# Norms two and four of a hybrid decoder step: squares in two parts, a root on ScalarE, state updates in other chunks, y in pairs

## The chip, the core and the metric

The kernel runs on one core of one Trainium2 chip. The core has a matrix engine (TensorE, PE in the profile, with its weight loads as PEld), VectorE (DVE), ScalarE (ACT), GpSimd (POOL) and SyncE (SP). Each takes its instructions in a fixed order from its own queue, and they wait for each other by semaphores; SP, ACT and POOL also issue DMAs. The metric is the device time of one execution in microseconds (us).

## The reference

One layer of a decoder: two residual blocks, each with a norm before and a norm after. 256 prompt tokens and 64 sample tokens (8 sequences of 8) run together as NT = 320 columns. What matters here:

```
def rms_norm(x, w):
    y = xf * lax.rsqrt(jnp.mean(xf * xf, axis=-1, keepdims=True) + EPS)
    return y * w

h    = rms_norm(x, norm_mix_pre)                                  # norm one
mix  = concat(gate_out, ssm_out) @ w_out
x    = x + rms_norm(mix, norm_mix_post)                           # norm two
f    = conv_ffn(rms_norm(x, norm_ffn_pre), ..., w_up, w_down)     # norm three
x    = x + rms_norm(f, norm_ffn_post)                             # norm four, x is the output y
```

`ssm_out` comes from a state space mixer with four groups of heads, which also returns its states: one of the prompt, and one renewed state for each of the 8 sample sequences (`state * decay + outer products of the new tokens`). All of it is float32.

## The kernel before

**Layout.** Activations lie transposed: 16 blocks of 128 features (KD = 16), each 128 partitions by 320 tokens. A float32 product is done as three products of rounded parts (`accumulate`, lines 126 to 130): weight high times activation high (L128), weight high times activation low (L129), weight low times activation high (L130). Weights come in slabs of 512 KB (`slab`, L110): a DMA on SP's queue, a cast to the high half `whi` on ScalarE (L117), and the low half `wlo` on VectorE (L119), each with three buffers.

**Order of the work.** A planner lists the instructions of each engine ahead of time from its own estimate of durations and from priorities. `first()` gives a block the highest priority, slabs come next, and the rest follows the order in which it is written. `tc.issue_after(ins)` puts those instructions of a block that run on the engine of `ins` behind `ins` in that engine's queue. It orders the queue and adds no wait on other engines.

**Stages.** The input projection and both mixers run first. `chunk_out` (L198) adds a chunk of four blocks of a second product into the accumulator: per output block, 12 matmuls and one DVE addition (L210). `w_out` has 8 chunks, numbered 0 to 7, and a chunk takes some 28 us of TensorE. Between pairs of blocks it calls `tick`, `rate` times, which advances work from a list `bg` of generators: the head groups' state work (`ssd`), the norm of a group (`norm` in `heads_out`) and, with chunk 7, the last states.

**Norm two** (lines 967 to 986). `squares_of(sq2)` is called after each block of chunk 7: for blocks 0 to 12 ScalarE squares the block (L259) and POOL adds it to the total (L260); for blocks 13 to 15 ScalarE writes the square to PSUM (L274) and DVE adds it (L272, L276). `token_sums` (L236) sums the total over partitions with three small matmuls against ones (each is two passes), `rsqrt_of` (L219) finds the inverse root on DVE from a bit trick and three Newton rounds (11 instructions of three columns), `spread` (L245) turns the result into rows for all partitions with three transposes. Between the last matmul of chunk 7 and the sums stands `final`, the prompt state of group 3 (two passes on TensorE, L902; sum on DVE, L903; DMA on ScalarE's queue).

**The last sample states** (`renewals`, L810, group 3). For each of four steps i, two states: loads on SP (L713), `picked` on ScalarE (L793), `renewed` with POOL's products (L798), two matmuls (L802) and two DVE sums (L803), and `store_state` with two DMAs on ScalarE's queue (L808). The first two steps run with chunk 7, the third is issued around the sums of norm two, the fourth behind the up projection's first part.

**x1 and norm three** (lines 987 to 1016). `x1_ready` makes the new x block by block: scale by norm two (L1001, DVE), add the old x (L1002; DVE for the first two blocks, POOL after), split into `h_hi` (L320, ScalarE) and `h_lo` (L321, DVE). The up projection starts as blocks come; besides its 512 columns it takes 256 more from the other half (`more`) with two further PSUM banks. Squares for norm three are made on ScalarE and added in turn by POOL (`sq3`) and DVE (`sq3b`). They are read by `token_sums(sq3, sq3b)` (L1078), which TensorE meets between the halves of `ps_one`.

**Norm four and y** (lines 1100 to 1149). The last chunk of `ffn_w_down` calls `last`, which squares as above and scales the block (L1107). After the sums, `hand_over` copies x1 blocks into PSUM through TensorE with an identity (L1129, two passes a block), so that DVE can add them from there. `r4` is the spread in PSUM and `r4s` its copy in SBUF. Eight pairs of blocks follow: five on DVE, three (5, 6, 7) on POOL, and DMAs to y that take turns on SP's and ScalarE's queues.

Of the kernel before, what the change touches and what calls it, by code (L numbers as in the profile page):

```python
# [34 lines left out]
def hybrid_step(  # L35
# [116 lines left out]
    def project(w, c0, evac, width=512, spare=False, late=None, quiet=0, ready=None, small=0, after=None, ahead=1, rate=1, more=None):  # L152
# [26 lines left out]
        for i, (k0, nk) in enumerate(cuts):  # L179
            with tc.issue_after(there or after) if there or after and i > 1 else nullcontext():  # L180
                if ready and i + ahead < len(cuts):
                    there = ready(*cuts[i + ahead])
                if nk < 4:
                    part(rows_of(w, k0, nk, c0, 512), k0, nk, range(4))
                    if more and k0 % 4 == 2:
                        part(rows_of(w, k0 - 2, 4, more, 256), k0 - 2, 4, (4, 5))
# [48 lines left out]

    def token_sums(*sqs):  # L236
# [25 lines left out]
    def squares_of(total):  # L262

        held = []

        def step(nb):
            if nb < KD - 3:
                add_square(total, acc[:, nb, :], nb == 0)
                return
            with first():  # L270
                if held:
                    dve.tensor_tensor(out=total, in0=total, in1=held.pop(), op=ALU.add)  # L272
                held.append(misc("sq_ps")[:, :NT])
                act.activation(held[0], acc[:, nb, :], AF.Square)  # L274
                if nb == KD - 1:
                    dve.tensor_tensor(out=total, in0=total, in1=held.pop(), op=ALU.add)  # L276
        return step
# [61 lines left out]
    with ExitStack() as mctx:  # L339
# [336 lines left out]
        with tc.tile_pool(name="sd", bufs=1) as sd:  # L676
# [26 lines left out]
            def ssd(g):  # L703
# [92 lines left out]
                def renewed(i, st, bm):  # L796
                    for h in range(2):
                        pool.tensor_tensor(out=by_head(st[h]), in0=by_head(st[h]),  # L798
                                           in1=tote[:, h0:h0 + 8, 4 * h + i:4 * h + i + 1].to_broadcast([P, 8, 64]), op=ALU.mult)
                    for h in range(2):  # L800
# [5 lines left out]
                def store_state(i, st):  # L806
                    for h in range(2):
                        act.dma_start(o_ssm_s[4 * h + i, g], st[h])  # L808

                def renewals():  # L810
                    sts = [load_state(i) for i in range(2)]
                    yield
                    for i in range(4):
                        st = sts.pop(0)
                        made = renewed(i, st, picked(i))
                        if i == 2:
                            yield made
                        elif i < 2:
                            yield
                        store_state(i, st)  # L820
                        if i < 2:
                            sts.append(load_state(2 + i))

                for i in range(4):
# [6 lines left out]
                    if g < 3:  # L831
                        renewed(i, st, bm)
# [67 lines left out]
                def final():  # L900
                    ps = misc("fin_ps")
                    made = pe.matmul(ps, btok[:, 1, bs], x1d, start=True, stop=True)  # L902
                    dve.tensor_tensor(out=s1, in0=s1, in1=ps, op=ALU.add)  # L903
# [330 lines left out]
```

## Time and profile before

| what | us |
|---|---|
| median of 3 runs (1817.86, 1818.88, 1823.92) | 1818.88 |
| the profiled execution's own time | 1820.49 |
| its span, first to last instruction | 1818.8 |
| TensorE matmul busy | 1784.2 (98%) |
| VectorE busy | 1181.1 (65%) |
| ScalarE busy | 790.5 (43%) |
| GpSimd busy | 300.3 (17%) |
| PE idle from 470 to 780 | 6.4 |
| PE idle from 850 to 865 | 7.2 |
| PE idle from 1800 to the end | 11.5 |

"Busy" is the time in which the engine had an instruction of the program running; the idle time before an instruction is put down to what released it. PE's busy time counts matmuls in flight, and the granted clock stands beside it in the windows: at half clock a busy PE does half the work. The profile shows 24 loads of ScalarE's function tables (ACT_TABLE_LOAD), 1283 ns each; the last two are at 757.72 us (for SiLU) and at 923.41 us (for GELU).

### The profile page before, as it was taken

What the parts mean: (1) busy time and instruction counts of PE and PEld (TensorE: products, weight loads), DVE (VectorE), ACT (ScalarE), POOL (GpSimd) and SP (SyncE); (2) the same over time, 40 slices, a digit from 0 to 9 for tenths busy, and PEclk for the clock granted to TensorE, in tenths of its full rate; (3) what the DMA queues carried; (4) which work ended last, traced back from release to release, by engine and by line L of the source; (5) the groups of instructions that cost most, each with busy time, mean ns of one, the idle gap of its engine ahead of it and who ended that gap; (6) DMA issues with size and microseconds to landing.
All of it is one profiled execution on the core that took longest, in us unless ns stands there. A gap on an engine that the chain in (4) does not pass through costs nothing.

```text
span 1818.8 us, 31127 instructions
## 1 busy us (share of the span) xinstructions
PE 1784.2 (98%) x12189; PEld 1746.0 (96%) x12189; DVE 1181.1 (65%) x2046; ACT 790.5 (43%) x1094; POOL 300.3 (17%) x623
## 2 busy tenths in 40 slices
PE   8999999999999999998999999999999999999997
PEld 7999999999889799997999999999999999999996
DVE  4449664557977868676776465747566575656575
ACT  5444454334535445444554433333434343433334
POOL 2102200000331302103521010111101020101004
PEclk9999999999999999999999999999999999999999
DMA  8646545555566565555454545454445444454542
GB/s 266 187 141 185 174 133 152 156 155 176 201 190 190 171 190 176 151 170 180 150 161 152 152 151 152 152 153 152 153 150 154 146 154 146 154 150 152 151 154 93
DMA packets 222994, 294.65 MB, mean 162 GB/s; under 512 B 16736, under 2 KB 150464, under 8 KB 222656
## 3 DMA queue, kind: packets, MB, share of 16 engines
q1 hardware_dynamic: 210256, 269.72, 48.6%
q10 hardware_dynamic: 10448, 16.10, 2.4%
q0 software_dynamic: 2144, 6.85, 1.3%
q8 instruction: 96, 1.57, 0.4%
q14 instruction: 50, 0.41, 0.1%
HBM read 277.80 MB, written 14.82 MB: 161 GB/s over the span
## 4 chain that ended last, share of the span: by engine, by line
PE 87%; DVE 5%; DMA 3%; POOL 2%; ACT 1%; issue 1%; POOLq 0%; SPq 0%; ACTq 0%; DVEq 0%
PE ps L128 18%; PE ps L129 18%; PE ps L130 18%; PE pd L128 9%; PE pd L130 9%; PE pd L129 9%; DVE wlo L119 2%; DMA st<-in_state_ssm 1%; DMA cT<-in_x_tok 1%; PE y_ps L876 1%; ACT whi L117 1%; POOL acc_mix L1002 1%; DVE cs L861 0%; PE sg L640 0%; DVE cv L363 0%
## 5 line engine op out<-in xcount | busy, mean ns | idle before, releaser
L119 DVE TENSOR_TENSOR wlo<-wraw,whi 128x1024 fp32r<-128x1024 f32 (+1 forms) x474 | 588.0, 1241 | 448.2 <-ACT whi L117 445.5
L117 ACT CAST whi<-wraw 128x1024 fp32r<-128x1024 f32 (+1 forms) x474 | 494.1, 1043 | 727.0 <-PE ps L129 428.2
L128 PE MATMUL ps<-h_hi,whi 128*128 128x320 f32 x2528 | 787.5, 312 | 6.6 <-ACT whi L117 3.7
L130 PE MATMUL ps<-h_hi,wlo 128*128 128x320 f32 x2528 | 784.1, 310 | 3.5 <-DVE wlo L119 3.5
L129 PE MATMUL ps<-h_lo,whi 128*128 128x320 f32 x2528 | 783.3, 310 | 0.0
L128 PEld LDWEIGHTS ps<-h_hi,whi 128*128 128x128 f32 x2528 | 477.3, 189 | 12.0 <-ACT whi L117 4.4
L130 PEld LDWEIGHTS ps<-h_hi,wlo 128*128 128x128 f32 x2528 | 477.1, 189 | 5.7 <-DVE wlo L119 5.6
L129 PEld LDWEIGHTS ps<-h_lo,whi 128*128 128x128 f32 x2528 | 477.2, 189 | 0.7 <-issue 0.5
L130 PE MATMUL pd<-fhi,wlo 128*128 128x320 f32 x704 | 217.4, 309 | 0.0
L128 PE MATMUL pd<-fhi,whi 128*128 128x320 f32 x704 | 217.4, 309 | 0.0
L129 PE MATMUL pd<-flo,whi 128*128 128x320 f32 x704 | 217.4, 309 | 0.0
L128 PE MATMUL pd<-ohi,whi 128*128 128x320 f32 x448 | 140.2, 313 | 0.0
L129 PE MATMUL pd<-olo,whi 128*128 128x320 f32 x448 | 138.9, 310 | 0.0
L130 PE MATMUL pd<-ohi,wlo 128*128 128x320 f32 x448 | 138.6, 309 | 0.0
L128 PEld LDWEIGHTS pd<-fhi,whi 128*128 128x128 f32 x704 | 132.2, 188 | 0.0
L129 PEld LDWEIGHTS pd<-flo,whi 128*128 128x128 f32 x704 | 132.2, 188 | 0.0
L130 PEld LDWEIGHTS pd<-fhi,wlo 128*128 128x128 f32 x704 | 132.2, 188 | 0.0
L1056 POOL COPY ptf<-pad 128x2 f32<-128x2 f32 x88 | 21.1, 240 | 598.0 <-DVE pad L1044 597.5
L210 DVE TENSOR_TENSOR acc_ffn<-acc_ffn,pd 128x320 f32<-128x320 f32 x160 | 77.4, 484 | 38.8 <-PE pd L130 37.4
L128 PEld LDWEIGHTS pd<-ohi,whi 128*128 128x128 f32 x448 | 84.1, 188 | 2.8 <-issue 1.6
L130 PEld LDWEIGHTS pd<-ohi,wlo 128*128 128x128 f32 x448 | 84.1, 188 | 1.0 <-issue 1.0
L129 PEld LDWEIGHTS pd<-olo,whi 128*128 128x128 f32 x448 | 84.1, 188 | 0.4 <-issue 0.2
(286 smaller groups left out, 1582.6 us busy)
## 6 DMA issues: line engine op xcount, KB each, us to landing
wraw<-in_ffn_w_up SPq DMA_DIRECT2D x176, 512.0 KB, 3.7
wraw<-in_w_in SPq DMA_DIRECT2D x144, 512.0 KB, 3.7
wraw<-in_ffn_w_down SPq DMA_DIRECT2D x88, 512.0 KB, 3.5
wraw<-in_w_out SPq DMA_DIRECT2D x64, 512.0 KB, 3.5
st<-in_state_ssm SPq DMA_DIRECT2D x40, 256.0 KB, 3.8
out_ssm_state_sample<-st ACTq DMA_DIRECT2D x32, 256.0 KB, 3.6
cs<-dacs_d SPq DMA_DIRECT2D x16, 320.0 KB, 4.4
xr<-in_xT SPq DMA_DIRECT2D x4, 640.0 KB, 4.8
```

The lines of the kernel that those rows point to most:

```text
L117: act.copy(hi[:, :m], raw[:, :m])
L119: dve.tensor_tensor(out=lo[:, :m], in0=raw[:, :m], in1=hi[:, :m].bitcast(F32), op=ALU.subtract)
L128: pe.matmul(ps, whi, xhi, start=first, stop=False)
L129: pe.matmul(ps, whi, xlo, start=False, stop=False)
L130: return pe.matmul(ps, wlo, xhi, start=False, stop=last).ins
L210: dve.tensor_tensor(out=acc[:, nb, :], in0=acc[:, nb, :], in1=ps[:, :NT], op=ALU.add)
L876: pe.matmul(ps[64 * i:64 * i + 64, cols], w(hl), x(hl, m, cpx), tile_position=(0, 64 * i), **flags)
L1002: added.append((dve if kt < 2 else pool).tensor_tensor(out=a, in0=a, in1=xr[q][:, k, :], op=ALU.add).ins)
L1056: pool.tensor_copy(ptf[:, k, :], pad[:, 256:258])
```

## The change

It has five parts.

- **Squares.** `squares_of` now returns its step and a list `one`. Blocks 13 and 14 are squared into PSUM and added by DVE; the square of block 15 goes to an SBUF tile of its own. The sums over partitions are taken in two goes: first of the 15 blocks, then of the last block alone.
- **Root.** `rsqrt_by_root` takes the two sums: two DVE steps make mean plus EPS, ScalarE takes the square root, DVE the reciprocal, and one Newton round follows (three DVE steps). A first `Sqrt` of one column stands behind the square of block 0, so that the table is loaded there.
- **States.** `renewed` is split into `shrunk` (POOL) and `grown` (TensorE, DVE), with a tick between. Steps 0 and 1 run with chunk 6, step 2 and the products of step 3 with chunk 7; the matmuls of step 3 come right behind chunk 7 and its stores go out by POOL's queue. `final` is a generator: its matmul comes behind the sums, its DVE sum behind the root, its store (group 3) goes out by POOL's queue.
- **Third norm.** All sums of squares are on DVE, in one total `sq3`. The `more` slabs' DVE work stands behind the second x1 block (`held`).
- **y.** x1 blocks 0 to 10 are handed over and done on DVE, in pairs and one after the other, and go out by SP; blocks 11, 12 to 13 and 14 to 15 are done on POOL and go out by ScalarE's queue. `r4s` comes from a second spread.

```diff
+        with tc.issue_after(held[1]):
+            part(rows_of(w, k0 - 2, 4, more, 256), k0 - 2, 4, (4, 5))
...
+    def rsqrt_by_root(rest, ps, scale, rows=P):
...
+        dve.tensor_scalar(out=v, in0=rest, scalar1=scale, scalar2=EPS, op0=ALU.mult, op1=ALU.add)
+        dve.scalar_tensor_tensor(out=v, in0=ps, scalar=scale, in1=v, op0=ALU.mult, op1=ALU.add)
+        act.activation(s, v, AF.Sqrt)
+        dve.reciprocal(r, s)
+        dve.scalar_tensor_tensor(out=t, in0=v, scalar=-0.5, in1=r, op0=ALU.mult, op1=ALU.mult)
+        dve.tensor_tensor(out=t, in0=t, in1=r, op=ALU.mult)
+        rsqrt_ins.append(dve.scalar_tensor_tensor(out=r, in0=t, scalar=1.5, in1=r, op0=ALU.add, op1=ALU.mult).ins)
+        return r
...
     def squares_of(total):
-        held = []
+        one, held = [], []
         def step(nb):
             if nb < KD - 3:
                 add_square(total, acc[:, nb, :], nb == 0)
+                if nb == 0:
+                    act.activation(tp.tile([P, 1], F32, name="root_there", bufs=1), total[:, 0:1], AF.Sqrt)
                 return
             with first():
-                if held:
-                    dve.tensor_tensor(out=total, in0=total, in1=held.pop(), op=ALU.add)
-                held.append(misc("sq_ps")[:, :NT])
-                act.activation(held[0], acc[:, nb, :], AF.Square)
-                if nb == KD - 1:
-                    dve.tensor_tensor(out=total, in0=total, in1=held.pop(), op=ALU.add)
-        return step
+                if nb < KD - 1:
+                    held.append(misc("sq_ps")[:, :NT])
+                else:
+                    one.append(tp.tile([P, NT], F32, tag="sq", name="sq", bufs=2))
+                act.activation((one or held)[-1], acc[:, nb, :], AF.Square)
+                if nb > KD - 3:
+                    dve.tensor_tensor(out=total, in0=total, in1=held.pop(0), op=ALU.add)
+        return step, one
...
                 def renewals():
                     sts = [load_state(i) for i in range(2)]
                     yield
                     for i in range(4):
+                        st, bm = sts.pop(0), picked(i)
+                        shrunk(i, st)
+                        yield
+                        made = grown(st, bm)
+                        store_state(i, st, act if i < 3 else pool)
                         if i < 2:
                             sts.append(load_state(2 + i))
+                        yield made
...
             finish(norm)
+            bg.append(chain(repeat(None, 1), islice(rest[0], 4)))
             chunk_out(w_out, 6, *res[2], False, rate=2)
...
-            bg.append(chain(repeat(None, 4), islice(rest[0], 2)))
-            chunk_out(w_out, 7, *res[3], False, squares_of(sq2))
+            bg.append(islice(rest[0], 3))
+            squares, one = squares_of(sq2)
+            chunk_out(w_out, 7, *res[3], False, squares)
...
                 with tc.issue_after(pd_last[-1]):
-                    made = rest[1]()
+                    made = next(rest[0])
                 with tc.issue_after(made):
-                    ps = token_sums(sq2)
-                r = rsqrt_of(ps, 1.0 / D, 3)
+                    most = token_sums(sq2)
+                with tc.issue_after(sums_ins[-1]):
+                    ps = token_sums(*one)
+                with tc.issue_after(sums_ins[-1]):
+                    made = next(rest[1])
+                r = rsqrt_by_root(most, ps, 1.0 / D)
                 behind = rsqrt_ins[-1]
                 with tc.issue_after(behind):
-                    made = next(rest[0])
+                    next(rest[1])
...
-            project(ffn_w_up, 0, None, late=up0, ready=x1_ready, after=behind, ahead=1, more=DFF)
-            sq3b = tp.tile([P, NT], F32, tag="pv", name="sq3b", bufs=4)
-            with tc.issue_after(added[11]):
+            project(ffn_w_up, 0, None, late=up0, ready=x1_ready, after=behind, ahead=1, more=DFF, held=added)
+            with tc.issue_after(added[15]):
                 for kt in range(KD):
-                    add_square((sq3, sq3b)[kt % 2], acc[:, kt, :], kt < 2, (pool, dve)[kt % 2], ("pv", 4))
-            with tc.issue_after(behind):
-                for _ in rest[0]:
-                    pass
+                    add_square(sq3, acc[:, kt, :], kt < 1, dve, ("pv", 4))
...
-        r = rsqrt_of(token_sums(sq4), 1.0 / D, 3)
-        hand_over((mm, "mm"), 0, 1)
+        with tc.issue_after(pd_last[-1]):
+            most = token_sums(sq4)
         with tc.issue_after(sums_ins[-1]):
-            hand_over((mm, "mm"), 2, 3)
-        r4 = spread(r)
-        r4s = fp.tile([P, NT], F32, name="r4s")
-        act.copy(r4s, r4)
+            made = hand_over(banks, 0)
+        with tc.issue_after(made):
+            ps = token_sums(*one)
+        r = rsqrt_by_root(most, ps, 1.0 / D)
+        with tc.issue_after(sums_ins[-1]):
+            made = hand_over(banks, 1, 2)
+        with tc.issue_after(made):
+            r4 = spread(r)
+            r4s = fp.tile([P, NT], F32, name="r4s")
+            spread(r, r4s)
+        hand_over(banks, 3)
+        hand_over(more, 4, 5)
+        hand_over(banks, 6, 7, 8, 9, 10)
+        made = None
+        for ks in [slice(k, k + 2) for k in range(0, 10, 2)] + [slice(10, 11)]:
...
+            with tc.issue_after(made) if made else nullcontext():
+                dve.tensor_tensor(out=f, in0=f, in1=r4.unsqueeze(1).to_broadcast([P, n, NT]), op=ALU.mult)
+            for k in range(n):
+                made = dve.tensor_tensor(out=f[:, k, :], in0=f[:, k, :], in1=x1p[ks.start + k], op=ALU.add).ins
+            sp.dma_start(o_y[:, ks, :], f)
+        for ks in (slice(11, 12), slice(12, 14), slice(14, 16)):
...
+            pool.tensor_tensor(out=f, in0=f, in1=r4s.unsqueeze(1).to_broadcast([P, n, NT]), op=ALU.mult)
+            pool.tensor_tensor(out=f, in0=f, in1=x1[:, ks, :], op=ALU.add)
+            act.dma_start(o_y[:, ks, :], f)
```

59 lines of the change are left out of this document (25 added, 34 removed).

## The prediction

> **What bounds the kernel now.** I read the page first, then the windows, the chain of waits, and each engine's timeline where TensorE is not full. The page gives TensorE 98% of the span (1784.2 of 1818.8 us), so a change can win only where it idles or runs at a low clock. The windows show two such places (columns: stretch and its length; busy us and instructions of PE, PEld, DVE, ACT, POOL; granted clock; DMA share, GB/s):
>
> ```profile
> 850.00:855.00 5.00, 2.54 (x14) 1.71 (x12) 2.71 (x6) 1.74 (x3) 4.19 (x4) 0.99 0.85 300
> 855.00:860.00 5.00, 2.50 (x8) 1.78 (x8) 3.72 (x14) 0.00 (x0) 0.00 (x0) 0.50 0.49 159
> 860.00:865.00 5.00, 2.76 (x10) 2.36 (x11) 4.60 (x11) 1.73 (x4) 0.04 (x1) 0.50 0.25 96
> 865.00:870.00 5.00, 5.00 (x24) 4.90 (x23) 4.05 (x8) 2.15 (x5) 4.12 (x5) 0.65 0.45 139
> 1800.00:1819.00 19.00, 7.48 (x25) 4.49 (x25) 10.00 (x27) 0.91 (x2) 9.08 (x6) 0.78 0.35 138
> ```
>
> The first is norm two, between chunk 7 of `w_out` and the up projection; the second is norm four with the output y. These are their rows in the timelines (start, length, engine, line, tiles, forms, idle time before and what ended it):
>
> ```profile
> 851.52 1.02 PE L902 MATMUL fin_ps<-xde,btok 128*128 128x512 f32 x2
> 856.49 1.44 PE L241 MATMUL tsum<-ones,sq 128*128 128x1 f32 x6 [3.95 <-DVE sq L276]
> 860.15 0.90 PE L249 MATMUL spread<-ident,rs_r 128*128 128x128 f32 x3 [1.16 <-DVE rs_r L230]
> 863.14 1.97 PE L128 MATMUL ps<-h_hi,whi 128*128 128x320 f32 x6 [2.09 <-ACT h_hi L320]
> ...
> 848.38 1.06 POOL L798 TENSOR_TENSOR st<-st,tote 128x512 f32<-128x512 f32 x1 [3.85 <-DMA st<-in_state_ssm]
> 849.40 2.80 POOL L260 TENSOR_TENSOR sq<-sq,sq 128x320 f32<-128x320 f32 x2
> ...
> 852.23 0.49 DVE L272 TENSOR_TENSOR sq<-sq,sq_ps 128x320 f32<-128x320 f32 x1 [1.71 <-POOL sq L260]
> 854.58 1.46 DVE L119 TENSOR_TENSOR wlo<-wraw,whi 128x1024 fp32r<-128x1024 f32 x1 [0.47 <-DMA wraw<-in_ffn_w_up]
> 855.97 0.47 DVE L276 TENSOR_TENSOR sq<-sq,sq_ps 128x320 f32<-128x320 f32 x1
> ```
>
> POOL waited for a state's load, so its last two square sums came late; DVE, in order, waited for them with the last evictions behind it; then a slab's low half (`wlo`, 1.46) stood ahead of the last sum. From the start of the last projection matmul (851.38; call it T) to the first up matmul TensorE did 11.76 us of little.
>
> ```profile
> 1799.92 0.49 DVE L276 TENSOR_TENSOR sq<-sq,sq_ps 128x320 f32<-128x320 f32 x1 [0.51 <-ACT sq_ps L274]
> 1801.33 0.16 DVE L224 TENSOR_SCALAR rs_v<-tsum 128x3 f32<-128x3 f32 x1 [0.92 <-PE tsum L241]
> 1803.30 0.16 DVE L230 SCALAR_TENSOR_TENSOR rs_r<-rs_t,rs_r 128x3 f32<-128x3 f32 x1
> 1804.24 0.43 ACT L1136 COPY r4s<-spread 128x320 f32<-128x320 f32 x1 [3.76 <-PE spread L249]
> 1804.70 1.55 DVE L1143 TENSOR_TENSOR acc_ffn<-acc_ffn,spread 128x640 f32<-128x640 f32 x2 [1.24 <-ACT r4s L1136]
> ...
> 1812.37 1.53 POOL L1145 TENSOR_TENSOR acc_ffn<-acc_ffn,acc_mix 128x640 f32<-128x640 f32 x1
> ...
> 1813.93 0.36 SPq L1149 DMA_DIRECT2D out_y<-acc_ffn  x1
> ```
>
> At the end DVE waits 1.24 us for ScalarE's copy of the same bank, POOL finishes y last (1813.90), and SP's queue waits for that; two finished pairs stand behind it (issued at 1814.33 and 1814.88). With 3.0 us to landing (2.2 to 3.0 on this line) and 0.9 of closing that makes 1818.8.
>
> **Middle, step by step** (from T; the tail's last projection matmul started at 1798.58, so its rows price the same steps undisturbed). The last eviction runs at +0.35 to +0.84 (1798.93). Its square took 0.47 to SBUF; in the trace a weight cast (1.03, at 853.52) stood between the last two squares, and I keep it there: square done at +1.95 (without it +1.34). The sums of the other 15 blocks no longer follow it. Column sums to DVE 0.86 (1800.47 to 1801.33): +2.8. One DVE step 0.20; the root on ScalarE: no row of three columns, 0.23 for 128x32 (L439), and 0.16 is what the smallest DVE row takes, so 0.16 to 0.34 (L425, 160 columns), I take 0.25 with its hand-over; the reciprocal took 1.15 for 160 columns (L427), three columns lie between 0.16 and 0.32, I take 0.20; three DVE steps of 0.20: spread at +4.15. Removed are eight steps of 0.20 of the old chain. Then, as before, 0.94 to the first x1 step and 2.05 to the first matmul: +7.15. **Gain 11.76 - 7.15 = 4.6**; with the cast out of the way 5.2, with the sums at the half-clock price (1.44 for six, as at 856.49) 4.0.
>
> What moves: states 0 and 1 leave chunk 7 for chunk 6 (each: one pick on ScalarE 0.50, two POOL products 1.06, two matmuls 0.31, two DVE sums 0.68, two loads on SP, two stores on ScalarE), state 2 goes into chunk 7, state 3's products too; its two matmuls fill the start of the gap, and the prompt state's one product (two passes, 1.02) moves behind the sums, into the root's wait. In chunk 6 DVE was busy 15.64 of the 20 us from 800; 4 x 0.68 more still fits, and the low halves run two slabs (7 us) ahead of TensorE: nothing, up to 2.7 lost if that cover fails. The state loads wait on SP for their buffers (5.21 at 843.57) ahead of weight slabs; chunk 7 bore that without idle PE, so nothing, else up to 1.7 (5.2 less one slab of 3.5). Three stores go to POOL's queue: 0.55 of issue each (L534), 1.65 in all, where POOL idled 10.0 us before 864.96; nothing, 1.65 if they fall behind. The root's table is loaded behind the first square of each last chunk: 1.28 plus 0.2 on a ScalarE busy 3.9 of 10 us: nothing. The `more` slab's low half now follows the second x1 block on DVE, ahead of the first `h_lo`: 1.2 to 1.5, covered by the six matmuls that need `h_hi` alone (1.97); nothing, 1.5 if they don't come first.
>
> Third norm: seven POOL sums (1.10) go, and eight more DVE sums (0.49) come, less four state sums (0.68): DVE from 860 to 910 goes from 39.6 to 40.8 busy. ScalarE's squares keep their number. Six of twelve column matmuls go (1.46 to 0.83): **0.6 gained**. Between the last old sum (900.8) and its reader (910.82) lay 10 us; the longer chain takes 8 x 0.49 = 3.9 of it.
>
> Clock: half speed held from 854.9 to 868.5, 5.4 us of it under full work, where a matmul came every 0.267 us rather than 0.147: 2.4 us lost. I keep that loss (bounds: all of it regained, 2.4; or another 1.4 us of half speed, 0.6 lost). The Trainium skill, "TensorE: Matmul & The Clock Gate", Part 1, says that an idle window of some 3.4 us halves the clock and a busy one of that length restores it, on a free-running grid. The trace agrees: 13.6 us between drop and return is four such windows, and by that rule a gap with work inside may not drop at all.
>
> **Tail.** The sums of 15 blocks run behind the last matmul (+0.15 to +0.84), one hand-over 0.62, then the last block's sums at +1.5; DVE has them at +2.35, r at +3.6 (before +4.88), spread at +3.65. DVE starts at +4.4, for it has its own bank (before +6.12). r4s takes a second spread (0.35) and its copy: POOL starts at +5.3 (before +6.16). DVE's pair in the new order is 0.92 + 0.40 + 0.40 = 1.72 (1810.81, 1811.73, 1812.13); five of them and a single block (0.58 + 0.49) end at +14.05. POOL has five blocks at 1.54 a pair and pass: 7.7, +13.0 (before +15.3). SP carries only what DVE makes, ScalarE's queue only POOL's. Last issue +14.1, landing 2.2, closing 0.9: +17.1 against 20.2. **Gain 3.1**; 2.0 if DVE's dependent steps or the landing cost a microsecond more, 3.8 if the last 160 KB land in 1.5.
>
> **Sum:** 4.6 + 0.6 + 3.1 = 8.3. Against the profiled execution: 1818.8 - 8.3 = 1810.5 span, and its run of 1820.49 less 8.3 is 1812.2. That run stood 1.6 above the median of three, so I take the gain from the median: 1818.88 - 8.3 = **1810.6**. The bounds of prices and clock at their worst leave 2.0 + 4.0 + 0.6 - 0.6 = 6.0 of gain (1812.9), at their best 3.8 + 5.2 + 0.6 + 2.4 = 12.0 (1806.9); if the four covers failed as well, 7.5 more would be lost (2.7 + 1.7 + 1.6 + 1.5; 1820.4).
>
> **Rivals.**
> 1. *The gap gets too short to lose the clock.* For: the new gap holds some 3 us of work (two state matmuls, twelve sums, the prompt product, the spread); against: the tail lost its clock near 1803.8 though TensorE's rows fill 2.5 of the 4 us from 1800. Then 2.4 more: 1808.2.
> 2. *The middle is given back after the restart:* x1's chain on DVE (two x1 steps, low half, split) becomes the bound for the first slabs, as 0.9 us of waits for `wlo` near 890 hint. The tail's gain stays: 1818.9 - 3.1 = 1815.8.
> 3. *The root isn't hidden:* its table lacks Square or Copy, so ScalarE reloads in the path. No row shows that set; casts, squares and copies ran from 758 to 923 with no reload, which says only that other sets hold them. Price: a load before the root and one after it in each norm, 4 x 1.28 = 5.1: 1815.7. The Trainium skill, "ScalarE: Activation LUTs", section "What ACT_TABLE_LOAD costs", has 2.66 us a switch with a drain, by which it would be 1821.2; here the loads took 1.28 with 0.02 idle ahead of them, so the trace does not agree.
> 4. *Slower:* the third norm's sum is one serial chain of 15 at low priority on DVE, and TensorE meets its column sums after the first half of `ps_one`, some 47 us after the restart. It decides from one sum per 3.1 us (47/15); at one per slab (3.53) it ends 6 late, at one per 4.2 us 16 late, plus 2.4 of lost clock: 1810.6 + 18.4 = 1829. Against: the old seven DVE sums ran in 9 us.
>
> **Chances:** forecast 0.57, rival 1 0.13, rival 2 0.14, rival 3 0.07, rival 4 0.09. A measurement of this kernel tells about 0.3% (5.5 us) from no change: faster means below 1813.4. Faster 0.57 + 0.13 = 0.70, same 0.14 + 0.07 = 0.21, slower 0.09. Range 1807.0 (all at best) to 1817.5 (rivals 2 and 3 with 1.7 us to spare, or the forecast with most covers gone); left out are rival 4 and the edges.
>
> **What would show it.** Right: column sums about 2 us after T, the up projection 7 us after T; no POOL wait for `st` in the last 10 us of chunk 7; 26 table loads instead of 24; no PE idle at `tsum` near 905; y's last issue some 14 us after the last matmul, on SP. Wrong: table loads within the two norms, PE waiting for `wlo` or `h_lo` in the first 20 us after the restart, or for DVE at the third norm's sums, PE idle in chunk 6.

## The result

| kernel | median us | ratio to before, 95% interval |
|---|---|---|
| before (4 runs, 1817.86 to 1823.92) | 1818.55 | |
| after (4 runs, 1807.21 to 1810.50) | 1808.67 | 0.9940 [0.9918, 0.9961] |
| after, run again in five rounds | 1809.33 | 0.9944 [0.9932, 0.9956] |

The forecast was 1810.6. The profiled execution of the changed kernel took 1810.5, its span is 1808.8 against 1818.8.

To see where the 10.0 us are, cut the span at three points: T (start of the last projection matmul of chunk 7), the first up projection matmul (the gap ends), and the last matmul of `ps_other` (end of the first feed-forward group). From there to the last matmul both traces take 872.96 us, and then comes the tail.

| stage, us | before | after | gain | forecast |
|---|---|---|---|---|
| up to a matmul some 90 us ahead of T, ahead of every edit | 761.29 | 760.88 | 0.41 | 0 |
| from there to T (851.38 and 851.43) | 90.09 | 90.55 | -0.46 | 0 |
| gap, T to the first up matmul | 11.77 | 6.42 | 5.35 | 4.6 |
| restart to the last matmul of `ps_other` | 62.47 | 60.24 | 2.23 | 0.6 |
| on to the last matmul | 872.96 | 872.96 | 0 | 0 |
| tail, last matmul to the end | 20.21 | 17.75 | 2.46 | 3.1 |

The gain is 1.7 above the forecast's 8.3, and most of its parts are off. The 0.46 lost ahead of T is two state matmuls more that run there (six instead of four); the stage behind the restart holds two fewer, so 0.46 of its 2.23 is only moved. The rest of the 2.23 is 0.74 for the column sums and 1.4 for waits of TensorE that are gone, less 0.4 because half clock lasted 6.2 us in that stage and not 5.4. These are the windows of the changed kernel (columns as before: stretch and length; busy us and instructions of PE, PEld, DVE, ACT, POOL; clock; DMA share, GB/s):

```profile
850.00:855.00 5.00, 4.56 (x28) 3.56 (x27) 4.08 (x12) 2.06 (x4) 1.13 (x2) 1.00 0.49 164
855.00:860.00 5.00, 2.69 (x11) 2.45 (x12) 4.96 (x11) 2.44 (x6) 1.65 (x2) 0.72 0.28 107
860.00:865.00 5.00, 5.00 (x24) 5.00 (x23) 4.56 (x8) 2.92 (x7) 3.03 (x3) 0.59 0.49 126
865.00:870.00 5.00, 5.00 (x37) 5.00 (x36) 4.72 (x8) 2.72 (x4) 2.70 (x2) 1.00 0.52 127
```

At 860 TensorE is full again, where it did 2.76 us in the same five before. The clock still falls (0.59 of full speed from 860). The timelines of the middle (start, length, engine, line, tiles, form; idle time before and what ended it):

```profile
846.15 1.49 POOL L276 TENSOR_TENSOR sq<-sq,sq 128x320 f32<-128x320 f32 x1 [0.79 <-ACT sq L275]
848.00 0.88 POOL L276 TENSOR_TENSOR sq<-sq,sq 128x320 f32<-128x320 f32 x1 [0.36 <-ACT sq L275]
...
851.63 1.05 ACT L117 CAST whi<-wraw 128x1024 fp32r<-128x1024 f32 x1 [0.34 <-PE pd L129]
851.78 0.49 DVE L211 TENSOR_TENSOR acc_mix<-acc_mix,pd 128x320 f32<-128x320 f32 x1
852.58 0.46 ACT L294 ACTIVATE sq<-acc_mix 128x320 f32<-128x320 f32 x1
853.10 0.83 PE L257 MATMUL tsum<-ones,sq 128*128 128x1 f32 x6 [0.33 <-ACT sq L294]
854.16 0.20 ACT L245 ACTIVATE rs_s<-rs_v 128x3 f32<-128x3 f32 x1 [1.11 <-DVE rs_v L244]
854.40 0.18 DVE L246 RECIPROCAL rs_r<-rs_s 128x3 f32<-128x3 f32 x1 [0.27 <-ACT rs_s L245]
855.22 0.54 PE L265 MATMUL spread<-ident,rs_r 128*128 128x128 f32 x3 [0.32 <-DVE rs_r L249]
855.80 1.00 DVE L1031 SCALAR_TENSOR_TENSOR acc_mix<-acc_mix,prm,spread 128x320 f32<-128x320 f32 x2
857.85 1.97 PE L128 MATMUL ps<-h_hi,whi 128*128 128x320 f32 x6 [2.09 <-ACT h_hi L340]
```

POOL's last square sums stand right behind their squares (it had waited 3.85 us for a state load here), the last eviction starts at T + 0.35, and TensorE's wait of 3.95 us for the total of squares has become 0.33. What is left of any size is the 2.09 from the end of the spread to the first up matmul, which waits for the first `h_hi` and which the change does not touch. The tail:

```profile
1793.56 0.20 ACT L245 ACTIVATE rs_s<-rs_v 128x3 f32<-128x3 f32 x1 [0.52 <-DVE rs_v L244]
1795.42 0.82 DVE L1177 TENSOR_TENSOR acc_ffn<-acc_ffn,spread 128x640 f32<-128x640 f32 x1 [0.85 <-PE spread L265]
1796.25 2.36 POOL L1184 TENSOR_TENSOR acc_ffn<-acc_ffn,r4s 128x320 f32<-128x320 f32 x2 [8.05 <-ACT r4s L267]
1802.51 1.54 POOL L1185 TENSOR_TENSOR acc_ffn<-acc_ffn,acc_mix 128x640 f32<-128x640 f32 x1
1804.47 0.49 DVE L1179 TENSOR_TENSOR acc_ffn<-acc_ffn,x1p 128x320 f32<-128x320 f32 x1
```

With the last matmul at 1791.05, DVE starts y at +4.37, POOL ends at +13.0, DVE at +13.9, and SP issues the last DMA at 1804.99 (+13.94). It lands after 2.46 us, and 1.35 us more pass to the end.

### The profile page after: what moved, and what is told of

The parts are those of the page before. It is cut to its first block, busy times and chain, and to the rows that moved or that the text cites. A ratio compares the mean times of both kernels' runs of the same rounds, so it can differ in the third digit from the quotient of the medians.

```text
span 1808.8 us, 31156 instructions
## 1 busy us (share of the span) xinstructions
PE 1781.4 (98%) x12200; PEld 1743.8 (96%) x12200; DVE 1183.7 (65%) x2044; ACT 793.7 (44%) x1100; POOL 294.7 (16%) x619
## 4 chain that ended last, share of the span: by engine, by line
PE 89%; DVE 5%; DMA 3%; issue 1%; ACT 1%; POOL 1%; SPq 0%; ACTq 0%; DVEq 0%; POOLq 0%
PE ps L128 19%; PE ps L130 19%; PE ps L129 19%; PE pd L128 9%; PE pd L130 9%; PE pd L129 9%; DVE wlo L119 2%; DMA cT<-in_x_tok 1%; DMA st<-in_state_ssm 1%; PE y_ps L898 1%; DMA cs<-dacs_d 1%; DMA out_ssm_state_sample<-st 0%; DVE cv L383 0%; DVE cs L883 0%; PE sg L660 0%
```

## The experiments

T itself lies between 846.6 and 852.3 us in the traces of the twelve runs below. Most of that spread arises between the thousandth and the four-thousandth matmul of 320 columns, where nothing was edited, so a single span tells little below 5 us. The stages agree far better (the stretch of 872.96 is the same in all; the 90 us ahead of T take 90.54 to 90.56 with the new states and 90.07 to 90.09 with the old), and the verdicts go by them; the medians of five rounds stand beside. The stages that say something:

| run | gap | restart to end of `ps_other` | tail | median | ratio to before, 95% |
|---|---|---|---|---|---|
| before | 11.77 | 62.47 | 20.21 | | |
| again | 6.42 | 60.14 | 17.74 | 1809.33 | 0.9944 [0.9932, 0.9956] |
| e_root | 7.71 | 60.18 | 18.34 | 1811.29 | 0.9967 [0.9952, 0.9982] |
| e_squares | 7.04 | 60.12 | 18.16 | 1810.12 | 0.9949 [0.9938, 0.9961] |
| e_states | 7.34 | 59.73 | 18.10 | 1811.11 | 0.9951 [0.9939, 0.9963] |
| e_joint | 8.75 | 59.33 | 18.56 | 1813.01 | 0.9956 [0.9942, 0.9971] |
| e_held | 7.03 | 60.18 | 17.73 | 1809.58 | 0.9949 [0.9937, 0.9961] |
| e_y | 6.43 | 60.16 | 19.37 | 1811.73 | 0.9957 [0.9944, 0.9969] |
| e_third | 6.52 | 66.20 | 17.74 | 1816.01 | 0.9982 [0.9973, 0.9991] |
| e_third_late | 6.42 | 64.96 | 17.75 | 1813.52 | 0.9968 [0.9958, 0.9979] |
| b_third | 12.14 | 59.38 | 20.05 | 1814.94 | 0.9974 [0.9965, 0.9983] |
| e_warm | 6.42 | 60.18 | 17.75 | 1809.54 | 0.9948 [0.9936, 0.9960] |
| e_warm_dve | 6.42 | 58.19 | 17.63 | 1806.77 | 0.9928 [0.9916, 0.9940] |

The before of these batches had medians of 1818.9 to 1819.8.

### The changed kernel again

> The changed kernel once more, as the measure for the others. Both theories: 1808.7 us within 1.5; gap from the last projection matmul of chunk 7 to the first up matmul 6.4 us; from the last FFN matmul to the end 17.7 us. The half-clock stretch after the restart is set by a free-running grid, so it may differ from the 6.8 us of the first profile (3.4 to 10.2).

The stages came out within 0.1 us of the first trace. That bounds what a stage of one kernel can be read to.

### The root undone (e_root)

```diff
-        act.activation(s, v, AF.Sqrt)
-        dve.reciprocal(r, s)
+        dve.tensor_scalar(out=r.bitcast(I32), in0=v.bitcast(I32), scalar1=-0.5, scalar2=float(0x5F3759DF),
+                          op0=ALU.mult, op1=ALU.add)
+        for _ in range(3):
```

> The changed kernel with the bit trick and three Newton rounds on DVE in place of the root, and no early root. Theory: ten DVE steps of 0.196 stand where root, reciprocal and three steps took 1.2, so the spread comes 1.0 later in both norms: gap 7.4, tail 18.7, 2.0 us longer in all, 24 table loads. Rival (the hand-overs to ScalarE and back cost what they save): within 0.5 us.

One Newton round becomes three, and the early load of the table goes. Gap +1.29, tail +0.59: 1.9 in all, close to the 2.0 expected, but not in the expected parts. In the gap the spread starts 0.94 later (T + 4.72 for T + 3.78), which is the root's worth, and takes 0.90 us in place of 0.54, since here the clock fell to half at T + 4.1, ahead of the spread, and in the changed kernel at T + 5.8, behind it: 0.36 of the 1.29 is the clock's. In the tail the roots end 0.93 apart too, but in the changed kernel TensorE is still handing over blocks when the root is ready, and the spread starts 0.33 later. The root's table sits in the place meant for it; the trace of the changed kernel has two loads at L287, one at 826.28 and one at 1766.32, and none within either norm.

### The squares undone (e_squares)

```diff
-                    one.append(tp.tile([P, NT], F32, tag="sq", name="sq", bufs=2))
+                if nb == KD - 1:
+                    dve.tensor_tensor(out=total, in0=total, in1=held.pop(), op=ALU.add)
...
-                with tc.issue_after(sums_ins[-1]):
-                    ps = token_sums(*one)
```

> The changed kernel with the last square in PSUM and added by DVE into one total, and one set of column sums as before; root kept. Theory: each norm's sums wait for one more DVE addition (0.49 and its hand-over), and in the middle for the state sums ahead of it on DVE: gap 6.9 to 7.7, tail 18.1 to 18.3, 1.0 to 1.9 us longer. Rival (the hand-over of one block ahead of the sums eats what the early sums give): under 0.4.

Gap +0.62, tail +0.41, and -0.12 behind the restart: 0.91 in all, just under the theory's 1.0 to 1.9 and well above the rival's 0.4. One DVE sum and one wait more on the path.

### The states undone (e_states), and both (e_joint)

```diff
-            bg.append(chain(repeat(None, 1), islice(rest[0], 4)))
             chunk_out(w_out, 6, *res[2], False, rate=2)
...
-            bg.append(islice(rest[0], 3))
+            bg.append(chain(repeat(None, 4), islice(rest[0], 2)))
...
```

`renewals` and `final` are the old ones. `e_joint` has this and the old squares.

> The changed kernel with the last sample states and the prompt's last state back where they were. Theory (the late POOL sums behind the state products were the larger part of the old gap): POOL waits again for a state's load near the end of chunk 7, the DVE sums of blocks 13 and 14 come after 852, and the gap grows from 6.4 to about 8.3 us; with two state matmuls back on TensorE's path after the restart (0.65) and two fewer in chunk 7 (0.43) the run is 2 to 3 us longer. Rival (the squares apart and the root make the whole gain in the middle): gap at most 6.9, time within 0.8.

Gap +0.92, between the two expectations; 0.30 of it is the spread at half clock (0.85 us), as in e_root. POOL's wait for the state load is back in the trace of e_states, 3.19 us of the old 3.85:

```profile
842.99 1.06 POOL L818 TENSOR_TENSOR st<-st,tote 128x512 f32<-128x512 f32 x1 [3.19 <-DMA st<-in_state_ssm]
844.00 2.70 POOL L276 TENSOR_TENSOR sq<-sq,sq 128x320 f32<-128x320 f32 x2
...
846.74 1.08 DVE L296 TENSOR_TENSOR sq<-sq,sq_ps 128x320 f32<-128x320 f32 x2 [0.37 <-POOL sq L276]
847.74 0.48 DVE L211 TENSOR_TENSOR acc_mix<-acc_mix,pd 128x320 f32<-128x320 f32 x1
```

But with T at 846.64 the last eviction (the row at 847.74) comes only 0.75 later than in the changed kernel, since the last block's square no longer needs the total. So the new squares take up most of that wait.

The gap isn't the whole account. Without the states' part the 90 us ahead of T are 0.46 shorter, and the stage behind the restart is 0.51 shorter although it holds the two state matmuls again. Together with the gap that is nothing lost (-0.05). Part of it is the clock, which came back 3.9 us into the stage and not 6.2; with half clock from T + 5.8 to T + 12.6, as in the changed kernel, an estimate from these figures is 0.4 lost (gap 0.62, stage 0.25, less 0.46). The tail is 0.35 longer, but its engines run as in the changed kernel, and 0.31 of the 0.35 passes after the last landing, for a reason that no run shows. So the rival's time (within 0.8) fits the stages, and the theory's 2 to 3 us does not; the medians, 1.8 apart, are too coarse to decide.

> The kernel after with the states' part and the squares' part of the second norm both undone (root and the cast behind the square are kept; fourth norm's squares undone too). Gap from T to the first up matmul: 6.42 in the changed kernel, 7.34 with the states' part undone alone, 7.04 with the squares' part undone alone, 7.71 without the root, 7.03 without the cast's wait. Theory (the two cover the same stall: GpSimd's wait for a state load makes the total of the early squares late, and the last square taken apart gives that total slack, so either alone hides most of it): 9.0 to 10.2, since 11.77 less 1.29 (root) less 0.61 (cast) is 9.87. Rival (the parts simply add up): 6.42 + 0.92 + 0.62 = 7.96, so 7.7 to 8.2.

Gap 8.75, that is +2.33 where the two alone add to 1.54: they do cover each other, but less than expected (9.0 to 10.2). Here too the spread ran at half clock, so 0.36 of the 2.33 is the clock's and 1.97 is theirs. In the whole (gap, tail +0.81, stage behind the restart -0.91, ahead of T -0.47) the two are worth 1.8. How e_joint, with the new root, still gains 3.02 in the gap on the kernel before is seen in its rows, with T at 852.32:

```profile
855.41 0.49 DVE L294 TENSOR_TENSOR sq<-sq,sq_ps 128x320 f32<-128x320 f32 x1 [0.81 <-ACT sq_ps L292]
855.95 0.83 PE L256 MATMUL tsum<-ones,sq 128*128 128x1 f32 x6 [2.46 <-DVE sq L294]
856.82 0.16 DVE L243 TENSOR_SCALAR rs_v<-tsum 128x3 f32<-128x3 f32 x1 [0.32 <-PE tsum L256]
```

The last sum starts at T + 3.09, and before at T + 4.59. Of these 1.50 us, 1.05 are the `wlo` of before (1.46, at 854.58), which stood there between the last square, done at 854.89, and its sum at 855.97; in e_joint it is held back and DVE is free when that square ends. The other 0.45 is POOL, whose last early sum ended that much later before. From the sum to the first root step before took 2.00 us and e_joint 1.41: the six column matmuls took 1.44 at half clock, and 0.83 at full. The last 0.94 is the root. So the 5.35 of the gap are 0.94 root, 1.97 squares and states, 1.05 the slab's low half, 0.45 POOL's lateness that e_joint did not bring back, and 0.95 that the column sums (0.59) and the spread (0.36) gained by running ahead of the fall of the clock.

### The `more` slab's low half not held back (e_held)

```diff
-                        with tc.issue_after(held[1]):
+                        with nullcontext():
```

> The changed kernel without the order for the further slab, whose low half (1.23) then stands on DVE between the two steps that make the mean. Theory: the mean is ready about 0.8 us later (the low half ends 0.8 after the last block's sums come), gap 7.2, and DVE is 1.2 us lighter after the restart, which TensorE at half clock does not need: 0.8 us longer. Rival (the low half ahead of h_lo delays the restart as much): same within 0.3.

Gap +0.61, and nothing after the restart. The `wlo` that stood ahead of the last sum before now stands at 851.16, where it delays the root's DVE steps: 0.61 with the new sums, and by the rows above 1.05 with the old, whose last sum stood behind it. The second figure is read from two traces that differ in more than this, not from a run of its own.

### The old order of y (e_y)

```diff
+        for i, q in enumerate((5, 0, 1, 6, 2, 3, 7, 4)):
+            on = pool if q in by_pool else dve
+            ...
+            (sp, act)[i % 2].dma_start(o_y[:, ks, :], f)
```

The new sums and root stay.

> The changed kernel with the old ending of y (ten blocks on DVE, six on POOL, one spread, r4s copied from the same bank, outputs in turn on two queues), root and squares kept. Theory: DVE starts 0.45 later behind ScalarE's copy, POOL ends at +15 rather than +13 and two finished pairs wait behind it on SP: tail 19.0 (18.7 to 19.4), 1.3 us longer, gap unchanged. Rival (the order of y does not matter, the gain of the tail is the earlier spread): tail 17.7 to 18.2.

Tail 19.37, as the theory has it, so y's order (with the second spread for `r4s`) is worth 1.63 of the tail's 2.46; with e_root (0.59) and e_squares (0.41) that makes 2.63.

### No loss of the clock (e_warm)

```diff
+                with tc.issue_after(spread_ins[-1]):
+                    ps = misc("warm")
+                    for _ in range(2):
+                        pe.matmul(ps, ones, prm[:, :512], start=True, stop=True)
```

The extra product is read by nobody.

> The changed kernel with two matmuls of constants (128x512, two passes each, some 1.7 us) behind the spread of norm two, in the 2.1 us in which TensorE waits for x1; their result is not used. Theory (half clock after the restart costs 2.4 to 2.8 us and comes from too little work in a window of 3.4 us): the granted clock stays 1.00 through the restart in most runs, 2.4 us shorter. First rival (x1's chain becomes the bound at full clock): clock 1.00, but TensorE waits for h_hi or h_lo after the restart, under 1 us shorter. Second rival (the clock falls anyway): the two matmuls take 3.4 us and the up projection starts 1.3 later.

The clock stayed at full speed and nothing came of it, which is the first rival: the stage after the restart took 60.18. TensorE's waits between 850 and 915 in that run (releaser: us in total, times, longest):

```profile
PE ps L130 <- DVE wlo L119: 1.3, 1, 1.3
PE ps L128 <- ACT h_hi L341: 0.4, 1, 0.4
...
PE ps L129 <- DVE h_lo L342: 0.2, 1, 0.2
```

The first is none in the changed kernel's first trace and 0.5 in its repeat: at 885.63 TensorE stands behind x1's chain, the work of DVE, ScalarE and POOL that makes x1 and its parts, with the low halves of the weights between. Half clock under full work lasted 6.2 us in the changed kernel, 2.8 in its repeat and 0 here, and the stage took 60.24, 60.14 and 60.18. The `wlo` in question ended 26.85, 26.88 and 26.92 us after the first up matmul in the three: the chain keeps its pace whatever TensorE's clock, and a faster TensorE only waits in it. In the changed kernel's first trace TensorE came to that `wlo` 0.97 after its end, so 6.2 us of half clock is about as much as the chain hides.

This holds for the changed kernel, and not for all. In e_states, e_joint and b_third (half clock 3.9, 2.9 and 3.3 us) TensorE meets no wait for weights or x1 in the stage, so nothing there hides the clock.

### The third norm undone (e_third, e_third_late), and alone (b_third)

```diff
-            with tc.issue_after(added[15]):
+            with tc.issue_after(added[11]):
...
-                    add_square(sq3, acc[:, kt, :], kt < 1, dve, ("pv", 4))
+                    add_square((sq3, sq3b)[kt % 2], acc[:, kt, :], kt < 2, (pool, dve)[kt % 2], ("pv", 4))
```

> The changed kernel with the third norm's squares added in turn by POOL and DVE into two totals, as before. Theory: six more column matmuls on TensorE's path, 0.6 to 0.7 us longer, and the sums stay early either way. Rival (the 1.2 us of waits for the low half near 890 came from two engines sharing the squares): those waits return, 1.8 us longer.

The stage grew by 6.0 us, where the theory had 0.6 to 0.7 and the rival 1.8. Undone from the changed kernel, the part costed at 0.6 holds more than the whole gap gained. TensorE's waits from 843 to 925 in e_third:

```profile
PE ps L130 <- DVE wlo L119: 2.4, 3, 1.4
PE ps L128 <- ACT whi L117: 2.3, 2, 2.0
```

Both are none in the changed kernel. Why the weights are late is seen in ScalarE's timeline of e_third:

```profile
884.87 1.04 ACT L117 CAST whi<-wraw 128x1024 fp32r<-128x1024 f32 x1
885.81 0.90 ACT L275 ACTIVATE sq<-acc_mix 128x320 f32<-128x320 f32 x2
889.30 0.47 ACT L275 ACTIVATE sq<-acc_mix 128x320 f32<-128x320 f32 x1 [2.59 <-POOL sq L276]
890.76 1.19 ACT L275 ACTIVATE sq<-acc_mix 128x320 f32<-128x320 f32 x3 [0.99 <-POOL sq L276]
891.85 1.03 ACT L117 CAST whi<-wraw 128x1024 fp32r<-128x1024 f32 x1
```

and in the changed kernel's:

```profile
884.12 1.03 ACT L117 CAST whi<-wraw 128x1024 fp32r<-128x1024 f32 x1
886.52 1.01 ACT L275 ACTIVATE sq<-acc_mix 128x320 f32<-128x320 f32 x2 [1.37 <-DVE sq L276]
888.59 1.00 ACT L275 ACTIVATE sq<-acc_mix 128x320 f32<-128x320 f32 x2 [1.07 <-DVE sq L276]
889.49 1.04 ACT L117 CAST whi<-wraw 128x1024 fp32r<-128x1024 f32 x1
```

The next cast comes 7.0 us after the last one, not 5.4: it stands in ScalarE's queue behind squares, and these wait until POOL has read one of the four square buffers. Besides, the early release puts POOL's sums between its x1 adds:

```profile
874.18 1.86 POOL L276 TENSOR_TENSOR sq<-sq,sq 128x320 f32<-128x320 f32 x1
876.00 1.12 POOL L1032 TENSOR_TENSOR acc_mix<-acc_mix,xr 128x320 f32<-128x320 f32 x1
877.09 1.13 POOL L276 TENSOR_TENSOR sq<-sq,sq 128x320 f32<-128x320 f32 x1
878.17 0.87 POOL L1032 TENSOR_TENSOR acc_mix<-acc_mix,xr 128x320 f32<-128x320 f32 x1
```

> The kernel after, with the third norm's squares in two totals again, one of GpSimd and one of VectorE, but released behind the last x1 and not behind the twelfth. With the early release the stage after the restart took 66.20 us, with the changed kernel's way 60.24. Theory 1 (the early release is the cost: GpSimd's sums get in among its x1 adds, which are late already, and the casts of the next weights stand in ScalarE's queue behind squares whose buffers GpSimd has yet to free): 60.8 to 62.0, that is 60.2 and six more column matmuls (0.7), with no wait of TensorE over 0.5 us before 890. Theory 2 (GpSimd's sums of 0.9 to 1.9 us are the cost wherever they stand, by the buffers): 63.5 or more, with waits for whi or wlo between 886 and 900.

64.96: with the release moved and POOL still in it, 1.24 us came back and 4.7 stayed. The second theory holds: GpSimd's part in the sums is the cost, more than their place, and the first theory's "no wait over 0.5 before 890" falls with a wait of 1.3 us for `whi` near 885. ScalarE waits for `sq` of POOL in this run too (1.07, 1.28 and 1.20 us between 884 and 890). A part of the 4.7 is a second fall of the clock at 888.4, for 3.4 us, that no other run has: up to 1.5 us at 0.267 for 0.147 a matmul, which would leave 63.4. What GpSimd's sums cost has two ways that these runs don't part: the buffers and ScalarE's queue, and VectorE, whose own seven sums took 0.85 us each beside them, against 0.49 in the changed kernel.

> The kernel before with the third norm's part alone: the sixteen sums of squares on VectorE into one total, released behind the last x1, six column matmuls instead of twelve. Stages as in the other runs: T to the first up projection matmul (11.77 us before), from there to the last matmul of ps_other (62.47 before, 60.24 after, 66.20 in the kernel after with this part undone). Theory (its worth hangs on the other parts: in the kernel before, the late start and 13.7 us of half clock give the x1 chain time that it lacks once the up projection starts 5 us sooner): gap 11.6 to 11.9; the stage shrinks by the six column matmuls (0.7) and at most by the two waits for wlo (1.5): 60.2 to 61.8. Rival 1 (the part is worth about 6 us in any kernel): 57 or less. Rival 2 (it moves nothing but the columns, as the prediction has it): 61.7 to 61.9 with both waits for wlo still there.

In the kernel before, the part alone gained 3.09 us in this stage. Both waits for `wlo` are gone (1.4 with what follows them), the columns give 0.74, and half clock under full work lasted 3.3 us instead of 5.4, which is some 0.95 more. That last is where the clock happened to return, and no work of the part; its own 2.1 lie within the theory's 0.7 to 2.2 and far below rival 1's 6. Rival 2, the prediction's 0.6, falls here as well. The medians have it 4.8 us faster than before (0.9974 [0.9965, 0.9983]); the stages, with a gap 0.37 longer, have 2.9. So the worth of this part grew from 2.1 to 6.0 once TensorE started 5 us sooner.

### A version that beats both (e_warm_dve)

```diff
-    added.append((dve if kt < 2 else pool).tensor_tensor(out=a, in0=a, in1=xr[q][:, k, :], op=ALU.add).ins)
+    added.append(dve.tensor_tensor(out=a, in0=a, in1=xr[q][:, k, :], op=ALU.add).ins)
```

It has e_warm's two matmuls too.

> The kernel with two idle-time matmuls of 512 columns behind the spread, in which the clock did not fall in the middle but TensorE then waited 1.9 us for x1's chain (stage after the restart 60.18), and with all sixteen x1 adds on VectorE where fourteen were GpSimd's. Theory (GpSimd's adds cost VectorE nearly as much as doing them itself: wlo takes 1.6 to 1.9 us and h_lo 1.16 beside one, 1.22 and 0.54 without; and each adds a hand-over between engines): VectorE's load stays about the same, the waits between 865 and 897 shrink below 0.5 us, stage 58.3 to 59.5. Rival (VectorE, busy 6.5 to 7.0 us of every 7 there, can't take 14 adds of 0.4 to 0.5 us more): 60.2 to 66, with more waits for wlo or h_lo. If the stage is shorter by a us or more at no loss elsewhere, this kernel is faster than both.

Stage 58.19, 2.0 us less than with either the changed kernel or e_warm, and 1806.77 us: 13.0 below before. Groups from 860 to 898 in e_warm (mean ns of one behind the busy us):

```profile
L1037 POOL TENSOR_TENSOR acc_mix<-acc_mix,xr 128x320 f32<-128x320 f32 x14 | 16.2, 1177 | 10.9 <-DVE acc_mix L1036 10.9
L119 DVE TENSOR_TENSOR wlo<-wraw,whi 128x1024 fp32r<-128x1024 f32 x9 | 13.6, 1509 | 0.4 <-ACT whi L117 0.4
L342 DVE SCALAR_TENSOR_TENSOR h_lo<-acc_mix,prm,h_hi 128x320 fp32r<-128x320 f32 x15 | 11.4, 779 | 1.0 <-ACT h_hi L341 1.0
L1036 DVE SCALAR_TENSOR_TENSOR acc_mix<-acc_mix,prm,spread 128x320 f32<-128x320 f32 x13 | 6.4, 539 | 0.0
```

and in e_warm_dve:

```profile
L119 DVE TENSOR_TENSOR wlo<-wraw,whi 128x1024 fp32r<-128x1024 f32 x11 | 13.3, 1218 | 0.6 <-ACT whi L117 0.6
L342 DVE SCALAR_TENSOR_TENSOR h_lo<-acc_mix,prm,h_hi 128x320 fp32r<-128x320 f32 x13 | 6.5, 546 | 1.6 <-ACT h_hi L341 1.6
L1036 DVE SCALAR_TENSOR_TENSOR acc_mix<-acc_mix,prm,spread 128x320 f32<-128x320 f32 x11 | 5.5, 540 | 0.0
L1037 DVE TENSOR_TENSOR acc_mix<-acc_mix,xr 128x320 f32<-128x320 f32 x12 | 5.2, 483 | 0.0
```

With GpSimd at the adds a `wlo` took 1509 ns on average and an `h_lo` 779; without, 1218 and 546. Inside e_warm it is the same split: from 855 to 900 the five `wlo` that run beside an add took 1.74 us on average and the six others 1.22, the nine such `h_lo` 0.94 and the seven others 0.54. VectorE took the adds over and was still busy for no longer: 32.0 of the 35 us from 862, against 32.8. An add took 483 ns there and 1177 on GpSimd. TensorE waited 0.5 us for `wlo` in place of 1.3. The adds on VectorE without the two extra matmuls were not run, so how the 2.0 us would look with the clock falling stays open.

## Why the prediction was right, and where it was not

**The total** was 1.9 us off the median (1810.6 against 1808.67), with the forecast mechanism in both norms. Its terms were off by +0.75 (gap), +1.63 (third norm, with 0.46 that only moved there), -0.46 (ahead of T, not in the sum at all) and -0.64 (tail); 0.41 more came ahead of every edit. That they partly cancel is luck, and so is it that 1808.67 lies nearer to rival 1's 1808.2: the clock fell, against that rival.

**The gap, 4.6 forecast, 5.35 measured.** The steps hold in order and nearly in size: square done at T + 1.61 (forecast 1.95; the cast kept in front of it started at +0.20, right after the square before), sums at DVE +2.54 (2.8), spread +3.79 (4.15), root 0.20 and reciprocal 0.18 (0.25 and 0.20). So the spread came 0.36 sooner than forecast. The second error, 0.36 too, is the step from the spread to the first x1 step: the prediction took 0.94 from the row at half clock, and at full clock it took 0.58. The 2.05 to the matmul came out as forecast. By the runs, the 5.35 are the root (0.94), squares and states together (1.97), the `wlo` now held back (1.05), POOL's lateness (0.45) and full clock for the column sums and the spread (0.95). The prediction had the last only for the column sums, as a bound ("at the half-clock price 4.0"): the clock fell at T + 3.5 before, T + 5.8 in the changed kernel and T + 4.1 in e_root and e_third, so how much of it a run gets is in part luck (e_third's spread lost 0.10 again).

**"Third norm ... 0.6 gained": the step that failed.** The prediction counted DVE's busy time and the column matmuls and stopped there. What the engines' sums cost others was not in it: POOL holds the square buffers that ScalarE needs, ScalarE's next casts stand behind those squares, and TensorE behind the casts. The sign was there in the trace of before, the waits for `wlo` near 890 and 895 that rival 2 mentions; ScalarE stood 1.02 and 1.03 us for `sq3b` and POOL's `sq` in the same place. Measured, the part is worth 2.1 alone and 6.0 with the rest. Its serial chain was not late (rival 4): the last sum ended at 897.5 and TensorE read it at 903.13, 5.6 us later, where the prediction had 10 less 3.9.

**Rival 2, "given back after the restart", was the right mechanism** for the kernel without that part, as far as it goes: e_third wins 5.25 in the gap and loses 3.73 in the stage behind. Half of TensorE's waits there are for `wlo` (2.4), as the rival has it, and half for ScalarE's casts (2.3), which it does not name. The prediction had gap and third norm as separate items; they are one.

**Clock, "I keep that loss".** Behind the restart it was no cost. The changed kernel runs 6.2 us of full work at half clock, more than before (5.4), and e_warm without any takes as long, because x1's chain is the bound there. Ahead of the restart it was one: the 0.95 above. Rival 1's 2.4 us were not there to be had in this kernel; with a shorter chain as well, e_warm_dve gained 2.0. The Trainium skill, "TensorE: Matmul & The Clock Gate", Part 1, section "What's actually happening", has a free-running window of 3413 ns: the stretches at half clock in the middle were 3.4, 6.8, 10.2 and 13.7 us, so the trace agrees. With TensorE's rows filling some 3.5 of the 6.3 us from the last projection matmul to the first up matmul the clock still fell, as the tail of before had hinted; with two more matmuls (1.88 us) it stayed, in both traces that have them (e_warm, e_warm_dve), where it fell in the other twelve.

**Tail, 3.1 forecast, 2.46 measured.** On the engines it holds to 0.2 (last issue +13.94 for +14.1, POOL's end +13.0 for +13.0). The miss is behind the last issue: 2.46 to land and 1.35 to close, against 2.2 and 0.9. Why the closing is longer, no run shows.

**What was costed at nothing.** In the changed kernel DVE was busy 17.57 us of the 20 from 800 and TensorE 20.00, with no wait of TensorE from 800 to 850; no POOL wait for `st` ahead of norm two; POOL's store issues (1.15 for two, at 853.16) in a stretch where it had nothing else. No `wlo` stood ahead of the first `h_lo` (857.98; the first `wlo` behind the restart came at 862.36). All four covers held. What the prediction left out is that the two state matmuls moved ahead of T cost TensorE 0.46 there, and save as much behind. Rival 3 falls: 26 loads, at the places forecast, 1283 ns each.

## What to carry to other kernels

When a stall ahead of a stage is cut, look first at which engine has no slack in that stage, and read every small wait there as the start of the next bound: here 0.9 us of waits for weights became 4.7. Judge a move by every stage that it touches: undoing the states' part cost 0.92 us in the gap and gave 0.97 back on its two sides, the clock included. Price a side task by whom it holds up through shared buffers and in-order queues, not by its own engine's busy time. A second engine for element-wise sums is no help where its operands and the first engine's get in each other's way: time the first engine's instructions with and without it.

## What the runs showed of the hardware

- A GpSimd add slows VectorE by about as much as the add would take there: in e_warm a `wlo` beside one took 1.74 us against 1.22 and an `h_lo` 0.94 against 0.54, in the sum some 0.44 us for each of the 14 adds, where an add on VectorE takes 0.48. A step that reads one operand from PSUM (L1036) took 0.54 either way. The Trainium skill, "SBUF — State Buffer", section "SBUF: two separate sides", says that a VectorE instruction with two SBUF operands and a GpSimd instruction lock each other out of a shared pair of ports. The trace agrees: it is the two instructions with two operands in SBUF that grew, and GpSimd's own add went from 0.87 to as much as 1.86 us.
- A half clock costs nothing where TensorE is not the bound: 0, 2.8 and 6.2 us of it gave stages of 60.18, 60.14 and 60.24. On a serial path it costs with the shortest matmuls too: six column sums took 1.44 us against 0.83, a spread 0.90 against 0.54.
- After a wait the first matmul of 320 columns shows 0.41 us in place of 0.31, and the pipelined rhythm of 0.147 starts anew, so a wait costs some 0.1 us more than its length.
- The runs differ by up to 5.7 us at T, most of it ahead of every edit, while the stages behind it repeat to 0.1.
